# Two-layer attention and expert network on one core: transposes, values and output transposes a unit apart, and the layer 1 queries and keys projected earlier

## The chip, the cores and the metric

The kernel runs on one core of a Trainium2 chip, as one program in one launch. The metric is the device time of that launch in microseconds (us), as the median of several runs. The engines are TensorE (PE; its weight loads are shown apart, as PEld), VectorE (DVE), ScalarE (ACT), GpSimd (POOL) and SyncE (SP), whose queue issues nearly all transfers.

## The reference, cut to what matters

256 latent tokens and 256 context tokens of width 1024 go through two layers. Each layer is a modulated norm, a mixer with attention, an output projection with a gated residual, and then a network of 16384 experts, which takes most of the time and which the change leaves alone. Layer 0 mixes by neighbourhood attention (8 heads) beside window attention (8 heads); layer 1 by latent attention (8 heads, queries and keys made from small normed vectors) beside differential attention (4 heads, each the difference of two softmaxes and a norm of its own):

```python
# layer 0, head by head
p = softmax(q @ k.T * scale + bias)          # latents see latents and context, context sees context
y = p @ v
# layer 1, latent heads ("c")
q = rmsnorm(cq, gq) @ w_uq;  kv = rmsnorm(ckv, gkv) @ w_ukv
y_c = softmax(q_mla @ k_mla.T * 96**-0.5) @ v
# layer 1, differential heads ("d")
o1, o2 = softmax(q1 @ k1.T / 8) @ v, softmax(q2 @ k2.T / 8) @ v
y_d = rmsnorm(o1 - lam * o2, g) * (1 - lam_init)
```

## The kernel before, in words

All of it is float32 or a float32 made of two parts: a product with weights is three matmuls (`mm3`, L191 to L193: high by high, high by low, low by high). Weights come as one stream in the order of use: `take` starts the load of the blocks to come on SP's queue (L162) and has the next block split into its two parts by ACT (L167) and DVE (L168). The split parts have six buffers, three pairs.

**Layer 1, projections** (`mixer1`). First come the shared rotary key (block `("cdin", 0)`) and `proj_n("ckv")`, which keeps four PSUM banks, one for each block of 128 tokens. PSUM has eight banks: four single ones under the tag `b`, which `self.ps()` hands out, and two pairs under `s2`, which in the mixers hold the scores. A loop over the four token blocks then norms what lies in those banks: a square on ACT (L605, L608), a factor by DVE and POOL (`rstd`, L309 and L311), the scaling on DVE (L607, L610) into `nat`. Eight transposes of `nat` (L229, `p<-ck,nat`) and their copies follow, then the projections of the differential queries `dq` (four blocks of 24 matmuls with 256 columns) and keys `dk` (four blocks with 512 columns), each into a bank from `self.ps()`, copied and rotated (`rope`, L378, with the rotation's matmul L389 and DVE's L391 to L393 coming one block later), then the values `dv` and the products of the normed latents.

**Attention.** A unit is a pair of heads (one differential head in "d") by 128 queries: 32 units in layer 0, 16 in layer 1. A unit goes through `unit_s` (scores of both heads into one `s2` pair; head 0 uses rows 0 to 63 of the PE array and head 1 rows 64 to 127; L527 in layer 0, L707 and for the rotary part L713 in layer 1), `unit_p` (maximum on DVE, L443 or L446, exponentials on ACT, L454), `unit_n` (division by the sum, DVE) and `unit_y`. `unit_y` transposes the probabilities (`flip`, L229, `p<-ck,P`, four transposes into one bank, copied to SBUF as `PT` by ACT, L479, or for the second head by DVE, L477), multiplies them by the values (L560 in layer 0; L739 for "c" and L745 for "d" in layer 1) and writes the result in two parts. A "d" unit goes on: square on ACT (L749), factor on DVE and POOL, scaling on DVE (L751, tile `o`), another transpose on PE (L229, `p<-ck,o`), and the two parts by ACT and DVE (L755 to L757).

The units are pipelined in program text: iteration i issues `unit_s` of i, `unit_p` of i-1, `unit_n` of i-2 and the whole `unit_y` of i-3. Between them a filler hands in pieces of the modulation vectors of later use (L245, L260, L269, 512 KB weight blocks from SP's queue): one piece an iteration in layer 0, two in layer 1, both ahead of `unit_p`. The tile framework then fixes one order for each engine: the program text is its preference, an instruction that it expects to be ready may go ahead of one that isn't, and on the chip each engine follows that order. After the last unit `out_proj` multiplies by the output weights, blocks 0 and 1 with the rows of the first kind of heads ("a" or "c"), blocks 2 and 3 with those of the second.

Of the kernel before, what the change touches and what calls it, by code (L numbers as in the profile page):

```python
# [18 lines left out]
PSUM = bass.MemoryType.PSUM  # L19
# [17 lines left out]
YLAG = (3, 3)  # L37
# [38 lines left out]
class Phase:  # L76
    """a pool whose tags have a set number of buffers"""
# [13 lines left out]
class Kernel:  # L91
# [103 lines left out]
    def proj_t(self, key, hh, hl, c=512, **kw):  # L195
        """[128 columns, c tokens] in PSUM"""
        if key in self.pre:
            return self.pre.pop(key)
        w = self.take(key, **kw)
        p = self.ps()  # L200
        if not isinstance(w, tuple):
            self.product8(p[:, :c], w)
            return p
        wh, wl = w
        for k in range(8):
            b = slice(k * 128, (k + 1) * 128)
            self.mm3(p[:, :c], wh[:, b], wl[:, b], hh[:, k, :c], hl[:, k, :c], k == 0, k == 7)
        return p

    def product8(self, out, w):  # L210
        """the same in float32, of the modulated norm kept whole"""
# [3 lines left out]
    def proj_n(self, name, hh, hl, width, nt=4):  # L215
        """natural layout: nt banks [128 tokens, width]"""
# [15 lines left out]
    def ada_mm(self, l, v, half, pool):  # L232
        """half of one modulation vector for both conditions, in rows 0 and 1 of each 32 as four partial sums"""
# [80 lines left out]
    def squares(self, x, half, ss, junk):  # L314
        """sum of squares of one half of a token block; with the second the factor of the norm"""
# [6 lines left out]
    def norm_mod(self, xs, rst, l, vsh, vsc, keys, mid=None):  # L322
        """modulated norm, transposed; the projections of keys go along with it"""
# [52 lines left out]
    def rope(self, x, p, perm, cos, sin, n):  # L376
        """x [128, n] from p in PSUM, its first 256 columns (the latents) rotated, the rotation after the next one"""
# [59 lines left out]
    def probs1(self, P, S, scale, sink=None, bias=None):  # L437
        """P [128, 2, nk] <- exp of the two heads' scores less their maximum; sums in sm"""
# [31 lines left out]
    def flip(self, x, nk, eng):  # L470
        """[128, 128 nk] -> [128 keys, nk, 128]"""
# [11 lines left out]
    def mixer0(self, xs, sq):  # L483
# [67 lines left out]
        def unit_y(kind, c, qs, ctx, P):  # L551
            nk = 2 if ctx else 4
            y = self.ps([128, 128])
            PT = [self.flip(P[:, s], nk, s) for s in range(2)]
# [14 lines left out]
        S, P, N = {}, {}, {}  # L569
        for i in range(n + YLAG[0]):  # L570
            if i < n:
                S[i] = unit_s(*units[i])
            next(filler, None)
# [4 lines left out]
            if 0 <= i - YLAG[0] < n:  # L578
                unit_y(*units[i - YLAG[0]], N.pop(i - YLAG[0]))
# [5 lines left out]
    def mixer1(self, xs, sq):  # L585
# [10 lines left out]
        # cq | ckv in natural layout  # L596
        ckv = self.proj_n("ckv", hh, hl, 384)
        nat = []
        for t in range(4):
# [12 lines left out]
            self.rope_end()  # L612
        qnh = self.m.t("h2", [128, 2, 256], R, name="qnh")
# [21 lines left out]
        # kr (replicated), dq, dk transposed  # L635
        dq, dk = [], []
        for b in range(4):
            if b % 2 == 0:
                pair = self.m.t("h2", [128, 2, 256], name="dqp")
            x = pair[:, b % 2, :]  # L640
            self.rope(x, self.proj_t(("cdin", 1 + b), hh, hl, c=256), *r64, 256)
            dq.append(x)
        for b in range(4):
            if b % 2 == 0:
                pair = self.m.t("q4", [128, 2, 512], name="dkp")
            x = pair[:, b % 2, :]
            self.rope(x, self.proj_t(("cdin", 5 + b), hh, hl), *r64, 512)
            dk.append(x)
# [4 lines left out]
        # latent queries, keys and values  # L653
# [77 lines left out]
        def unit_y(kind, c, qs, P):  # L731
            PT = [self.flip(x, 4, i) for i, x in enumerate(P)]
# [18 lines left out]
            nc.vector.tensor_scalar(o[:, 1, :], y, rs, None, op0=OP.mult)  # L751
            y2 = self.ps([128, 128])
# [6 lines left out]
        units = [(kind, c, qs) for c in range(4) for kind in "cd" for qs in range(2)]  # L759
        n = len(units)  # L760
        S, P, N = {}, {}, {}
        for i in range(n + YLAG[1]):
            if i < n:
                S[i] = unit_s(*units[i])
            for _ in range(2):
                next(filler, None)
# [4 lines left out]
            if 0 <= i - YLAG[1] < n:  # L771
                unit_y(*units[i - YLAG[1]], N.pop(i - YLAG[1]))
# [5 lines left out]
    def top16(self, V, X, a, b):  # L778
        """sorted top 16 of each a, b as scratch, interleaved over the lists"""
# [12 lines left out]
    def route_scores(self, l, T, nd, hh, hl):  # L792
        """sorted top 16 of each half key for the dense blocks; scores of a further block go to DRAM"""
# [44 lines left out]
    def route(self, sv, al):  # L838
        """experts i, j and gates of one token block; a generator, leaves them in self.rt"""
# [64 lines left out]
    def gates(self, go, ti, G):  # L904
        """gate matrix of 128 tokens -> DRAM; a generator"""
# [66 lines left out]
    def peer(self, l, xs, sq, nd):  # L972
        """nd dense token blocks; a further block, if any, goes by gathered rows; returns the pieces of f"""
# [51 lines left out]
        # routing and gate matrix, with the first products of the main loop in between  # L1025
# [72 lines left out]
        def gather(n0, n1, after=None):  # L1098
            """rows of slots n0..n1, not before after is there"""
# [70 lines left out]
        def pace(j):  # L1170
            """slots used by the end of iteration j, even in time"""
# [31 lines left out]
    def residual(self, l, f):  # L1203
        """x + g2 f, in a new mixer phase"""
# [28 lines left out]
    def run(self):  # L1233
# [35 lines left out]
        # lambda of the differential heads, gain of its norm  # L1269
# [30 lines left out]
        # final norm  # L1300
# [159 lines left out]
```

## Time and profile before

| what | value |
|---|---|
| time, median of 3 runs | 2739.62 us |
| lowest and highest run | 2728.51 and 2740.89 us |
| span of the profiled execution, the only time the page has of it | 2734.2 us |
| PE, PEld busy | 95%, 83% of the span |
| DVE, ACT, POOL busy | 69%, 46%, 19% |
| attention of layer 0 | from about 147 to 267 us |
| layer 1: wait after `proj_n("ckv")`; attention | from 1670 to 1679 us; from 1750 to 1860 us |

The profile is of one execution. A busy time counts an instruction from its start to its modelled end, and matmuls overlap, so a stretch in which PE is busy all the time can still have starts that lie further apart than they need to. In the timeline a row gives start, duration, engine, line, operation, output and inputs, shapes and how many instructions were merged; in brackets the idle time just before it and what ended that.

### The profile page before, as it was taken

To read this page: it belongs to the slowest core of one execution; us is meant where nothing else is said; L and a number is where in the kernel's file an instruction comes from. 1 tells how busy PE (TensorE), PEld (TensorE's weight loads), DVE (VectorE), ACT (ScalarE), POOL (GpSimd) and SP (SyncE) were. 2 spreads that over 40 slices of the span, in tenths; PEclk is the share of its full clock that TensorE was granted. 3 is DMA by queue.
4 is the path that set the end of the run, shared out by engine and by line. 5 is a ranking of instruction groups with operands and counts; after the bars stand their busy time and mean duration, and the time that the engine had idled before them with its cause. 6 is when DMAs were issued, how large, how long until landed. Compare 5 with 4: busy or idle time off the path is not lost.

```text
span 2734.2 us, 43073 instructions
## 1 busy us (share of the span) xinstructions
PE 2610.7 (95%) x16265; PEld 2261.8 (83%) x16265; DVE 1876.3 (69%) x3862; ACT 1267.3 (46%) x2201; POOL 529.2 (19%) x534
## 2 busy tenths in 40 slices
PE   7999998989999999999999989998999999999998
PEld 6866787878899999999899767757999899999986
DVE  4267588886977777777777765365997565555455
ACT  3255335997333333333333333343499444444454
POOL 0000000000045555566565530000000000000000
PEclk9999999999999999999999998998999999999999
DMA  7262323977688888888888862453467976565355
GB/s 291 101 216 86 111 88 128 287 235 246 232 313 311 308 315 306 316 299 321 294 309 288 275 225 75 164 195 113 144 215 242 318 267 210 208 211 214 130 193 183
DMA packets 240977, 614.15 MB, mean 225 GB/s; under 512 B 18384, under 2 KB 102608, under 8 KB 240768
## 3 DMA queue, kind: packets, MB, share of 16 engines
q1 hardware_dynamic: 203904, 477.17, 50.6%
q0 software_dynamic: 36864, 134.23, 13.9%
q8 instruction: 127, 2.08, 0.3%
q14 instruction: 82, 0.67, 0.1%
HBM read 558.90 MB, written 52.43 MB: 224 GB/s over the span
## 4 chain that ended last, share of the span: by engine, by line
PE 62%; DVE 6%; DMA 3%; ACT 3%; issue 2%; POOL 1%; SPq 0%; DVEq 0%; POOLq 0%; ACTq 0%
PE p L192 19%; PE p L191 19%; PE p L193 19%; DMA gr<-in_v,ix 1%; PE p L213 1%; PE s L707 1%; PE p L229 1%; DVE ws L168 1%; ACT stage L957 1%; ACT og L940 1%; DVE vs L168 1%; DMA sc<-sd 1%; PE p L954 1%; ACT ws L167 1%; PE p L245 0%
## 5 line engine op out<-in xcount | busy, mean ns | idle before, releaser
L167 ACT CAST ws<-w 128x1024 fp32r<-128x1024 f32 (+1 forms) x327 | 343.0, 1050 | 634.0 <-PE p L192 581.4
L168 DVE TENSOR_TENSOR ws<-w,ws 128x1024 fp32r<-128x1024 f32 (+1 forms) x327 | 397.5, 1216 | 267.7 <-ACT ws L167 267.4
L192 PE MATMUL p<-vs,w 128*128 128x512 f32 x1280 | 502.2, 393 | 7.5 <-DVE vs L168 7.5
L167 ACT CAST vs<-v 128x1024 fp32r<-128x1024 f32 x256 | 269.5, 1053 | 509.5 <-PE p L192 509.5
L191 PE MATMUL p<-vs,w 128*128 128x512 f32 x1280 | 499.6, 391 | 4.4 <-ACT vs L167 4.4
L193 PE MATMUL p<-vs,w 128*128 128x512 f32 x1280 | 501.6, 392 | 0.0
L191 PE MATMUL p<-hh,ws 128*128 128x384 f32 (+2 forms) x1336 | 472.2, 354 | 6.2 <-ACT ws L167 2.9
L193 PE MATMUL p<-hh,ws 128*128 128x384 f32 (+2 forms) x1336 | 466.0, 349 | 1.5 <-DVE ws L168 1.5
L192 PE MATMUL p<-hl,ws 128*128 128x384 f32 (+2 forms) x1336 | 466.6, 349 | 0.0
L168 DVE TENSOR_TENSOR vs<-v,vs 128x1024 fp32r<-128x1024 f32 x256 | 312.8, 1222 | 152.7 <-ACT vs L167 151.0
L191 PE MATMUL p<-hp,ws 128*128 128x256 f32 x1032 | 295.5, 287 | 1.8 <-ACT ws L167 1.1
L193 PE MATMUL p<-hp,ws 128*128 128x256 f32 x1032 | 292.8, 284 | 0.8 <-DVE ws L168 0.8
L192 PE MATMUL p<-hp,ws 128*128 128x256 f32 x1032 | 293.2, 284 | 0.0
L192 PEld LDWEIGHTS p<-vs,w 128*128 128x128 f32 x1280 | 241.3, 189 | 56.5 <-DVE vs L168 11.1
L193 PEld LDWEIGHTS p<-vs,w 128*128 128x128 f32 x1280 | 240.9, 188 | 53.7 <-DVE w L1153 3.0
L191 PEld LDWEIGHTS p<-vs,w 128*128 128x128 f32 x1280 | 241.1, 189 | 50.6 <-ACT vs L167 4.6
L191 PEld LDWEIGHTS p<-hh,ws 128*128 128x128 f32 x1336 | 255.0, 191 | 24.7 <-ACT ws L167 4.3
L192 PEld LDWEIGHTS p<-hl,ws 128*128 128x128 f32 x1336 | 254.6, 191 | 14.9 <-issue 0.5
L193 PEld LDWEIGHTS p<-hh,ws 128*128 128x128 f32 x1336 | 254.5, 190 | 13.1 <-DVE ws L168 2.0
L1123 DVE SCALAR_TENSOR_TENSOR acc<-gr,ga,acc 128x1024 f32<-128x1024 f32 x128 | 164.2, 1283 | 102.3 <-DMA gr<-in_v,ix 101.7
L1118 DVE SCALAR_TENSOR_TENSOR gr<-gr,hn 128x1024 f32<-128x1024 f32 x128 | 156.2, 1224 | 108.5 <-DMA gr<-in_u,ix 102.5
L311 POOL TENSOR_TENSOR rso<-rsm,mhalf 128x1 f32<-128x1 f32 x30 | 20.1, 671 | 1079.4 <-DVE rsm L309 1079.4
(267 smaller groups left out, 4127.6 us busy)
## 6 DMA issues: line engine op xcount, KB each, us to landing
w<-in_uT SPq DMA_DIRECT2D x256, 512.0 KB
v<-in_v SPq DMA_DIRECT2D x256, 512.0 KB
w<-in_ada_w SPq DMA_DIRECT2D x96, 512.0 KB
G<-stage SPq DMA_DIRECT2D x40, 1024.0 KB
g<-G SPq DMA_DIRECT2D x32, 768.0 KB
w<-in_wq SPq DMA_DIRECT2D x32, 512.0 KB
g<-G SPq DMA_DIRECT2D x32, 512.0 KB
w<-in_w_out SPq DMA_DIRECT2D x16, 512.0 KB
```

What stands on the lines that cost most here:

```text
L167: self.nc.scalar.copy(hi, raw)
L168: self.nc.vector.tensor_tensor(lo, raw, hi.bitcast(F), op=OP.subtract)
L191: m(out, lh, rh, start=start, stop=False)
L192: m(out, lh, rl, start=False, stop=False)
L193: m(out, ll, rh, start=False, stop=stop)
L213: self.nc.tensor.matmul(out, w[:, k * 128:(k + 1) * 128], self.h32[:, k, :], start=k == 0, stop=k == 7)
L229: self.nc.tensor.transpose(out, x, self.ck("ident"))
L707: nc.tensor.matmul(S[:, s, :], a[c][h, q], b[c][h, :], start=True, stop=kind == "d", tile_position=(64 * s, 0))
L940: nc.scalar.activation(og_[:, 1, g, :, b], oh[:, 1, g, :, b], AF.Copy, scale=gl[:, k:k + 1])
L954: nc.tensor.matmul(p[:, k, :], oh[:, 0, g, :, b], og_[:, w, g, :, b], start=(w == 0), stop=(w == 1))
L1118: nc.vector.scalar_tensor_tensor(t, t, 1.0, hn, op0=OP.mult, op1=OP.mult, accum_out=ga[:, 0, n:n + 1])
L1123: nc.vector.scalar_tensor_tensor(acc, t, ga[:, 0, n - 128:n - 127], acc, op0=OP.mult, op1=OP.add)
```

## The change

In both mixers `unit_y` is cut: `unit_f` does the transposes and copies for unit i-3, and the product with the values is done for unit i-4, an iteration later. In layer 1 the second transpose of "d" units and what follows it become `unit_o`, for unit i-5. The loops run one iteration (layer 0) and two iterations (layer 1) longer. Layer 0's filler is called between `unit_f` and `unit_y`; in layer 1 one of the two calls moves there. In layer 1 each head group goes "d" first, then "c". The projections of `dq` and `dk` go ahead of the transposes of `nat`; `dq` is accumulated in `s2` pairs (argument `p` of `proj_t`) and its tiles come from the tag `q4` in place of `h2`. The rest of the diff takes comments out.

```diff
-    def proj_t(self, key, hh, hl, c=512, **kw):
+    def proj_t(self, key, hh, hl, c=512, p=None, **kw):
...
-        p = self.ps()
+        p = self.ps() if p is None else p
...
 # mixer0
-        def unit_y(kind, c, qs, ctx, P):
+        def unit_f(kind, c, qs, ctx, P):
+            return [self.flip(P[:, s], 2 if ctx else 4, s) for s in range(2)]
+
+        def unit_y(kind, c, qs, ctx, PT):
             nk = 2 if ctx else 4
             y = self.ps([128, 128])
-            PT = [self.flip(P[:, s], nk, s) for s in range(2)]
...
-        for i in range(n + YLAG[0]):
+        for i in range(n + 4):
             if i < n:
                 S[i] = unit_s(*units[i])
-            next(filler, None)
             if 0 <= i - 1 < n:
                 P[i - 1] = unit_p(*units[i - 1], S.pop(i - 1))
             if 0 <= i - 2 < n:
                 N[i - 2] = unit_n(*units[i - 2], *P.pop(i - 2))
-            if 0 <= i - YLAG[0] < n:
-                unit_y(*units[i - YLAG[0]], N.pop(i - YLAG[0]))
+            if 0 <= i - 3 < n:
+                X[i - 3] = unit_f(*units[i - 3], N.pop(i - 3))
+            next(filler, None)
+            if 0 <= i - 4 < n:
+                unit_y(*units[i - 4], X.pop(i - 4))
...
 # mixer1, right after the loop over nat; the same lines go out behind the transposes of nat
+        dq, dk = [], []
+        for b in range(4):
+            if b % 2 == 0:
+                pair = self.m.t("q4", [128, 2, 512], name="dqp")[:, :, :256]
+                p2 = self.pq.t("s2", [128, 2, 512])
+            x = pair[:, b % 2, :]
+            self.rope(x, self.proj_t(("cdin", 1 + b), hh, hl, c=256, p=p2[:, b % 2]), *r64, 256)
+            dq.append(x)
+        for b in range(4):
+            if b % 2 == 0:
+                pair = self.m.t("q4", [128, 2, 512], name="dkp")
+            x = pair[:, b % 2, :]
+            self.rope(x, self.proj_t(("cdin", 5 + b), hh, hl), *r64, 512)
+            dk.append(x)
...
-                pair = self.m.t("h2", [128, 2, 256], name="dqp")
...
-        def unit_y(kind, c, qs, P):
-            PT = [self.flip(x, 4, i) for i, x in enumerate(P)]
+        def unit_f(kind, c, qs, P):
+            return [self.flip(x, 4, i) for i, x in enumerate(P)]
+
+        def unit_y(kind, c, qs, PT):
             y = self.ps([128, 128])
...
             nc.vector.tensor_scalar(o[:, 1, :], y, rs, None, op0=OP.mult)
+            return o
+
+        def unit_o(kind, c, qs, o):
+            if o is None:
+                return
+            dst = slice(qs * 128, qs * 128 + 128)
             y2 = self.ps([128, 128])
             self.transpose(y2, o[:, 1, :])
...
-        units = [(kind, c, qs) for c in range(4) for kind in "cd" for qs in range(2)]
+        units = [(kind, c, qs) for c in range(4) for kind in "dc" for qs in range(2)]
...
-        for i in range(n + YLAG[1]):
+        for i in range(n + 5):
             if i < n:
                 S[i] = unit_s(*units[i])
-            for _ in range(2):
-                next(filler, None)
+            next(filler, None)
             if 0 <= i - 1 < n:
                 P[i - 1] = unit_p(*units[i - 1], S.pop(i - 1))
             if 0 <= i - 2 < n:
                 N[i - 2] = unit_n(*units[i - 2], *P.pop(i - 2))
-            if 0 <= i - YLAG[1] < n:
-                unit_y(*units[i - YLAG[1]], N.pop(i - YLAG[1]))
+            if 0 <= i - 3 < n:
+                X[i - 3] = unit_f(*units[i - 3], N.pop(i - 3))
+            next(filler, None)
+            if 0 <= i - 4 < n:
+                Y[i - 4] = unit_y(*units[i - 4], X.pop(i - 4))
+            if 0 <= i - 5 < n:
+                unit_o(*units[i - 5], Y.pop(i - 5))
```

## Rows read from the trace of the kernel before

**Rows 1.** The page's part 1: busy us, share of the span, instructions.

```profile
PE 2610.7 (95%) x16265; PEld 2261.8 (83%) x16265; DVE 1876.3 (69%) x3862; ACT 1267.3 (46%) x2201; POOL 529.2 (19%) x534
```

**Rows 2.** The page's part 4: the chain that ended last, by engine.

```profile
PE 62%; DVE 6%; DMA 3%; ACT 3%; issue 2%; POOL 1%; SPq 0%; DVEq 0%; POOLq 0%; ACTq 0%
```

**Rows 3.** Stretches: length, busy us of PE, PEld, DVE, ACT, POOL; clock; DMA share.

```profile
180.00:216.00 36.00, 35.60 (x372) 22.43 (x370) 26.15 (x87) 18.12 (x59) 1.05 (x2) 1.00 0.55 196
...
1670.00:1680.00 10.00, 5.11 (x19) 3.03 (x17) 5.54 (x16) 3.07 (x13) 3.09 (x6) 0.62 0.24 83
...
1750.00:1842.00 92.00, 83.72 (x868) 48.49 (x867) 54.03 (x123) 37.98 (x99) 6.96 (x13) 0.97 0.59 213
1842.00:1860.00 18.00, 12.53 (x80) 9.09 (x79) 9.02 (x27) 7.49 (x22) 1.09 (x2) 0.78 0.08 31
```

**Rows 4.** Timeline of PE from the end of `proj_n("ckv")` into block 1 of `dq`.

```profile
1670.09 0.34 PE L193 MATMUL p<-ws,hl 128*128 128x384 f32 x1
1672.45 1.16 PE L389 MATMUL p<-kr,ck 128*128 128x256 f32 x2 [2.03 <-DVE nat L610]
...
1678.64 0.56 PE L191 MATMUL p<-hh,ws 128*128 128x256 f32 x1
...
1682.80 0.28 PE L191 MATMUL p<-hh,ws 128*128 128x256 f32 x1
1682.92 0.28 PE L192 MATMUL p<-hl,ws 128*128 128x256 f32 x1
```

**Rows 5.** Timeline of DVE there: the splits of the `dq` blocks' weights.

```profile
1667.21 1.23 DVE L168 TENSOR_TENSOR ws<-w,ws 128x1024 fp32r<-128x1024 f32 x1 [2.94 <-ACT ws L167]
...
1672.22 1.22 DVE L168 TENSOR_TENSOR ws<-w,ws 128x1024 fp32r<-128x1024 f32 x1
```

**Rows 6.** Groups of PE by line, 1750 to 1860 us: busy, mean ns, idle before.

```profile
L745 PE MATMUL p<-dv,PT 128*128 128x128 f32 x64 | 10.3, 309 | 3.7 <-ACT PT L479 3.6
...
L229 PE MATMUL p<-ck,o 128*128 128x128 f32 x8 | 2.9, 365 | 7.2 <-DVE o L751 5.4 <-DVE rc L467 1.6
```

**Rows 7.** Timeline of PE in the middle of layer 1's attention.

```profile
1785.36 0.60 PE L229 MATMUL p<-ck,P 128*128 128x128 f32 x4
1786.63 1.16 PE L745 MATMUL p<-dv,PT 128*128 128x128 f32 x8 [0.68 <-ACT PT L479]
```

**Rows 8.** Timeline of PE at the end of layer 1's attention.

```profile
1855.74 2.08 PE L745 MATMUL p<-dv,PT 128*128 128x128 f32 x8 [0.73 <-ACT PT L479]
1859.47 0.47 PE L229 MATMUL p<-ck,o 128*128 128x128 f32 x1 [1.66 <-DVE o L751]
...
1863.59 0.43 PE L191 MATMUL p<-ws,hh 128*128 128x512 f32 x1
...
1864.31 0.39 PE L191 MATMUL p<-ws,hh 128*128 128x512 f32 x1
1864.54 0.39 PE L192 MATMUL p<-ws,hh 128*128 128x512 f32 x1
```

**Rows 9.** Waits, 147 to 268 us: us in total, times, longest.

```profile
PEld p L560 <- ACT PT L479: 15.5, 27, 0.8
...
PE p L560 <- ACT PT L479: 1.3, 4, 0.4
```

**Rows 10.** Timeline of PE in layer 0's attention.

```profile
183.15 1.12 PE L527 MATMUL s<-qk 64*128 64x512 f32 x2
184.20 1.09 PE L560 MATMUL p<-PT,av 128*64 128x128 f32 x16
185.22 1.12 PE L527 MATMUL s<-qk 64*128 64x512 f32 x2
...
188.31 1.13 PE L527 MATMUL s<-qk 64*128 64x512 f32 x4
189.37 1.09 PE L560 MATMUL p<-PT,av 128*64 128x128 f32 x16
```

More of the change, by code (lines that the diff above doesn't have):

```diff
@@ L36 @@
 AGRP = (2,)
-YLAG = (3, 3)
 ADA_WAIT = 2
@@ L568, in mixer0 @@
         n = len(units)
-        S, P, N = {}, {}, {}
-        for i in range(n + YLAG[0]):
+        S, P, N, X = {}, {}, {}, {}
+        for i in range(n + 4):
             if i < n:
                 S[i] = unit_s(*units[i])
-            next(filler, None)
             if 0 <= i - 1 < n:
@@ L634, in mixer1 @@
         nc.vector.tensor_tensor(kvl, kf, kvh.bitcast(F), op=OP.subtract)
-        dq, dk = [], []
-        for b in range(4):
-            if b % 2 == 0:
-                pair = self.m.t("h2", [128, 2, 256], name="dqp")
[L640 to L648, printed above, removed]
         dv = [self.m.t("q4", [128, 2, 512], name="dv") for _ in range(2)]
@@ L757, in unit_y @@
             nc.vector.tensor_tensor(yl[:, 4 + c, dst], o[:, 2, :], yh[:, 4 + c, dst].bitcast(F), op=OP.subtract)
-        units = [(kind, c, qs) for c in range(4) for kind in "cd" for qs in range(2)]
+        units = [(kind, c, qs) for c in range(4) for kind in "dc" for qs in range(2)]
         n = len(units)
-        S, P, N = {}, {}, {}
-        for i in range(n + YLAG[1]):
+        S, P, N, X, Y = {}, {}, {}, {}, {}
+        for i in range(n + 5):
             if i < n:
                 S[i] = unit_s(*units[i])
-            for _ in range(2):
-                next(filler, None)
+            next(filler, None)
             if 0 <= i - 1 < n:
```

## The prediction

> **What bounds the kernel.** The page's part 1 comes first: PE is busy for 95% of the span [rows 1], and the chain that ended last is PE's for 62%, with DVE next at 6% [rows 2]. So a microsecond that PE gains in a mixer moves the end by about one, because the expert network behind it is PE's too. The change touches only the mixers, so the second view is the table of stretches: where does PE stand still, or run slowly, inside them? In layer 0's attention hardly at all (35.60 of 36 us busy, clock 1.00). In layer 1 there are three places: 1670 to 1680 us (5.11 of 10 us busy, clock 0.62), the attention (83.72 of 92) and its end (12.53 of 18, clock 0.78) [rows 3]. The timeline and the groups by line then say who waits for what there.
>
> **Part 1, `dq` and `dk` ahead of the transposes of `nat`.** PE's last `ckv` matmul starts at 1670.09 and ends at 1670.43; the first matmul of `dq` starts at 1678.64. That is 8.2 us, of which the first wait, 2.03 us, ends with DVE's L610, which gives a `ckv` bank back [rows 4]. What PE does in it has to be done later all the same: eight transposes, four of which take 0.60 us in a row at full rate [rows 7], so 1.2, and two rotation matmuls of 256 columns at 0.12 us, 0.2. Then the clock: from 1678.64 to 1682.80 PE starts 18 matmuls of `dq`, 0.23 us each, where later ones start 0.12 apart [rows 4]; the clock of this stretch is 0.62, a mixture of its two levels, 1.2 and 2.4 GHz [rows 3]. 18 times 0.12 is 2.2, so 2.0 us go here. Sum: 8.2 - 1.4 + 2.0 = 8.8 us.
>
> Can `dq` start at 1670.4? Its accumulation goes to `s2` pairs, which nothing holds before the first scores at 1750. The weights of its first two blocks are there: block 2's split ends at 1668.44 and block 3's at 1673.44 [rows 5], while block 3 would be wanted after two blocks of 24 matmuls at 0.12, at about 1676. The stream of weights keeps its order, so SP's queue sees the same loads; the moved transposes issue no DMA, and neither do the three activations and six DVE instructions behind them. Those were ahead of the ropes on ACT and DVE and are now behind them; their products are first wanted by `uq`, after `dv`, and the 96 matmuls of `dv` cover them. What is late next is the rotation of `kr`: if the fixed order has it early among `dq`'s matmuls, PE waits there for L610 as before, up to 2.03 us. Bounds: 0 (all of `nat` stays in front) and 8.8. I take 8.
>
> **Part 2, layer 1's attention.** Two waits are what the edit aims at. L745 stood 3.7 us behind the copies of its own transposes, and the "d" units' second transpose stood 7.2 us behind `o` and DVE [rows 6]. One instance: four transposes start at 1785.36 and are through at 1785.96, and the product starts at 1786.63, after 0.68 us of idling for the copy [rows 7]. In the new order a whole iteration lies between, some 5.75 us (92 us [rows 3] by 16 units), with the next scores and a piece of the filler; the norm of a "d" unit, for which PE idled 1.66 us at 1857.8 [rows 8], gets an iteration too. So 10.9 us of waits lose their cause. Against them stands the end, where no next unit covers: the last two units still go from transposes to copy to product, at 0.7 us each [rows 7], and part of the 5.4 us behind L751 comes from DVE being late with splits of output weights, which will make something else late: I leave 3 us. That "c" is now last takes the norm out of the last chain; its idle time is in the 10.9 already. The clock: between the starts at 1859.47 and 1863.59, 4.12 us, lie a transpose and nine matmuls of `out_proj`, 0.44 each, where later ones are 0.23 apart [rows 8]; nine times 0.21 is 1.9 us, given back if the end has fewer gaps. Sum: 10.9 - 3 + 1.9 = 9.8; I take 10. Bounds: 0, if each wait is replaced by one of the same length, and 12.8, with no rest.
>
> "d" ahead of "c" at the start is priced at nothing: PE is full with `uq` and `ukv` products while the "d" scores could already start. The longer loops add no instruction to PE; their last iterations have only the pieces that were in `unit_y`.
>
> **Part 3, layer 0.** PE's own idle time before L560 for a copy is 1.3 us; its weight loads waited 15.5 us in 27 places, mostly while an earlier matmul still ran [rows 9]. These bound the gain: 1.3 and 15.5. PE is busy for 35.60 of 36 us [rows 3], so the lower one is nearer; some product runs are also broken after the first pair because the second head's copy is late. I take 4. The filler moves by eight transposes; its loads from SP's queue and POOL's fills of its bias tile move with it and are wanted by nobody soon.
>
> One rule speaks for much more here. The Trainium skill (Perfetto Trace Analysis, Identifying the Most-Contended Engine) says that matmul busy time overstates how near PE is to its limit, and to judge by the share of weight loads. That share is 22.43 of 36 us [rows 3], so by this rule some 38% of the 120 us of this attention, 45 us as an estimate, would be open. The starts in the timeline don't bear it out: 16 products take 1.02 us and are followed at once [rows 10]. By the rule the sum would have room for 45 in place of 4; I keep 4.
>
> **Sum.** 8 + 10 + 4 = 22 us. The profiled span of 2734.2 would become 2712.2; that execution lies 5.4 us below the median of the runs, so against the median, 2739.6 - 22 = **2718 us**.
>
> **The rivals.**
>
> *The order run was already full* (0.08). Each engine's order is fixed ahead of the run with what is expected to be ready, and PE already slips scores between transposes and products [rows 10]. If that did all of it, the text's new order changes next to nothing: 2739. Against it: the waits of rows 6 are there in that order.
>
> *The waits stay, for want of banks* (0.22). The four `b` banks are unchanged, and a "d" unit now holds its three in three different iterations beside the filler's. Then parts 2 and 3 give nothing and part 1 its 8 or 9: 2731. For it: the wait in front of `dq` did end with a bank given back [rows 4]. Against it: in the attention the ones named are a copy and `o`, data and not a free bank [rows 6]. The Trainium skill has this as a rule (Perfetto Trace Analysis, Optimization Strategy): gaps that repeat can mean too little PSUM for the next tile. By that rule the gaps of rows 7 would outlive the change; the releasers named there speak for the data.
>
> *Slower: score pairs come apart* (0.10). The four score matmuls of a unit take 1.06 us together, as the heads use different rows of the array, but two of them alone take 1.05 also, so a pair with a product in between costs 1.05 us more [rows 10]. In the timeline 16 of layer 0's 32 units are split so (10 with 512 columns, 6 with 256, which I price at half), and 8 of layer 1's 16. The change gives PE products that are always ready, just what gets between. If all others split as well: 6 x 1.05 + 10 x 0.53 + 8 x 1.05, and 8 x 1.05 for L713: 28.4 us. With the gain of 22 that gives 2746, with part 1 alone 2760; it ends on the other side from 21 more split pairs on.
>
> *Faster still: they come together* (0.10). If the products no longer fall between heads, 18 x 1.05 and 6 x 0.53 us come back, 22.1: 2696.
>
> **How the numbers follow.** The forecast has a chance of 0.50 and, with part 1 from 7 to 9, part 2 from 3 to 13 and part 3 from 1 to 8, a range of its own of 2709 to 2728. The range has to reach the banks rival (2731) and the full order (2739), and 2704 takes in most of the forecast's upper bounds; what it leaves out is most of both split rivals, 0.15 to 0.2: 2702 to 2740. A measurement of this kernel can tell 0.5%, 13.7 us, from no change. Faster by that, below 2726: most of the forecast (0.44), the pairs together (0.10), a little of the banks (0.04): 0.58. Slower, above 2753: the pairs apart with less than 16 us gained, 0.08. The same: 0.34.
>
> **What would show it.** Part 1 is right if PE's starts go on within a microsecond after the last `ckv` matmul, with `dq` at 0.12 and the clock at 1.00 there; wrong if L389 or the transposes of `nat` come first. Part 2: L745 and `p<-ck,o` without idle time in the groups, and from the first scores to `out_proj` some 10 us less. Part 3: layer 0's attention 3 to 5 us shorter, product runs whole. The forecast fails if the runs of L527 and L707 by twos become many more or fewer, if the waits reappear at the scores (L707 behind L454) or at DVE, or if the time gained goes to waits for weights at the start of the experts.

## The result, and the profile after

The changed kernel takes **2692.13 us** (median of 4 runs, 2683.2 to 2698.7), the kernel before beside it 2737.36 us: ratio 0.9832, 95% interval 0.9807 to 0.9856. That is 45 us less, where 22 had been forecast; the time lies below the range of 2702 to 2740 and 4 us under the rival "they come together" (2696). The profiled execution has 2690.64 us and a span of 2688.9, 45.3 less than before. Its lines are numbered differently: the scores are L526 (layer 0) and L711 (layer 1; its rotary part is L717), the products L561, L745 ("c") and L751 ("d"), every transpose is L228, the filler L244, L259 and L268, the copies of the transposes L478 (ACT) and L476 (DVE).

First the page of the kernel after: part 1 (busy us, share, instructions) and the first line of part 4 (the chain that ended last).

```profile
PE 2574.6 (96%) x16265; PEld 2248.1 (84%) x16265; DVE 1870.6 (70%) x3862; ACT 1266.4 (47%) x2201; POOL 526.7 (20%) x534
...
PE 32%; DVE 3%; ACT 2%; issue 1%; DMA 0%; POOL 0%; SPq 0%; DVEq 0%; POOLq 0%; ACTq 0%
```

Against [rows 1] PE has the same 16265 instructions and the same share of a shorter span, but 36.1 us less of busy time. So most of the gain is busy time that went away, and only the rest idle time; the prediction had looked for it in idle time. (The chain's 32% is no fall in PE's weight: the shares listed now add up to 38%, those of [rows 2] to 77%.)

Where it went, by stages whose ends are read from PE's timeline: layer 0's attention (last matmul of `av` to the end of the last product), from the last `ckv` matmul to layer 1's first scores, and layer 1's attention (from there to the end of the last product):

```
us              before   after   difference   (part of the prediction)
up to av         143.4   142.4      -1.0
attention 0      123.7   111.5     -12.2      part 3, taken as 4
between         1383.6  1382.4      -1.2
ckv to scores     79.9    73.8      -6.1      part 1, taken as 8
attention 1      107.9    85.3     -22.6      part 2, taken as 10
the rest         876.4   874.0      -2.4
(first matmul of ckv to its last: 19.4 in both)
```

The two attentions as stretches, first of the kernel before, then of the kernel after (columns as in [rows 3]).

```profile
143.38:267.09 123.71, 121.31 (x1128) 73.71 (x1126) 94.42 (x327) 69.58 (x217) 2.10 (x4) 1.00 0.48 167
1749.95:1857.82 107.87, 95.78 (x944) 57.10 (x943) 62.55 (x147) 45.10 (x119) 7.51 (x14) 0.95 0.52 187
```

```profile
142.38:253.88 111.50, 104.17 (x1127) 68.08 (x1125) 91.38 (x327) 68.48 (x217) 2.11 (x4) 0.95 0.54 185
1729.55:1814.87 85.32, 81.91 (x946) 51.35 (x945) 61.30 (x150) 45.06 (x121) 8.04 (x15) 1.00 0.65 236
```

Layer 0's PE is busy for 17 us less in a stretch that is 12 shorter, with the same instructions. Layer 1 has 13.9 us less busy time, 8.7 less idle time, and the clock at 1.00 in place of 0.95. Which instructions got cheaper is in the groups by line (busy, mean ns, idle time before), here of the kernel before, layer 0 and then layer 1.

```profile
L527 PE MATMUL s<-qk 64*128 64x256 f32 (+1 forms) x124 | 43.5, 531 | 0.2 <-ACT P L454 0.2
...
L560 PE MATMUL p<-PT,bv 128*64 128x128 f32 x192 | 19.0, 284 | 1.4 <-ACT PT L479 0.9 <-DVE P L548 0.3
...
L560 PE MATMUL p<-PT,av 128*64 128x128 f32 x192 | 17.4, 283 | 0.5 <-ACT PT L479 0.4
...
L707 PE MATMUL s<-knp,qnp 64*128 64x512 f32 x32 | 15.9, 648 | 1.0 <-ACT P L454 1.0
...
L707 PE MATMUL s<-dkp,dqp 64*128 64x512 f32 x32 | 12.2, 703 | 0.5 <-ACT P L454 0.4
```

And the same groups of the kernel after, with those that answer to [rows 6].

```profile
L526 PE MATMUL s<-qk 64*128 64x256 f32 (+1 forms) x124 | 30.5, 544 | 1.1 <-ACT P L453 1.1
...
L561 PE MATMUL p<-PT,av 128*64 128x128 f32 x192 | 14.8, 292 | 0.8 <-DVE ar L250 0.7
...
L561 PE MATMUL p<-PT,bv 128*64 128x128 f32 x192 | 14.1, 283 | 0.1
...
L711 PE MATMUL s<-knp,qnp 64*128 64x512 f32 x32 | 11.3, 641 | 0.0
L751 PE MATMUL p<-dv,PT 128*128 128x128 f32 x64 | 9.1, 285 | 0.2 <-ACT PT L478 0.2
...
L711 PE MATMUL s<-dkp,dqp 64*128 64x512 f32 x32 | 9.0, 641 | 0.2 <-ACT P L453 0.2
...
L228 PE MATMUL p<-ck,o 128*128 128x128 f32 x8 | 2.4, 304 | 1.6 <-DVE ar L250 1.2 <-ACT o L755 0.4
```

The two waits of [rows 6] went from 3.7 to 0.2 and from 7.2 to 1.6 us, as meant. But the 124 score matmuls of layer 0 fell from 43.5 to 30.5 us busy at the same 0.53 to 0.54 us each: the same matmuls lie over each other more. The timeline of PE in layer 0's attention of the kernel after says how; it answers to [rows 10].

```profile
198.46 1.13 PE L526 MATMUL s<-qk 64*128 64x512 f32 x4
199.52 0.66 PE L228 MATMUL p<-ck,P 128*128 128x128 f32 x4
200.01 0.95 PE L268 MATMUL p<-ck,ar 128*128 128x2 f32 x8
200.89 1.09 PE L561 MATMUL p<-PT,av 128*64 128x128 f32 x16
201.91 0.70 PE L526 MATMUL s<-qk 64*128 64x256 f32 x4
```

The scores stand in fours, and the product stands behind the transposes and a piece of filler, not between two heads. In PE's fixed order the split pairs of layer 0 went from 10 (512 columns) and 6 (256) to 0 and 2, those of layer 1 from 8 to 2.

Last, PE's timeline behind `ckv`, which answers to [rows 4].

```profile
1655.70 0.33 PE L192 MATMUL p<-ws,hl 128*128 128x384 f32 x1
1655.87 0.28 PE L190 MATMUL s<-hh,ws 128*128 128x256 f32 x1
...
1656.70 0.28 PE L191 MATMUL s<-hl,ws 128*128 128x256 f32 x1
1658.06 0.67 PE L388 MATMUL p<-kr,ck 128*128 128x256 f32 x2 [1.08 <-DVE nat L613]
1658.38 0.47 PE L192 MATMUL s<-hh,ws 128*128 128x256 f32 x1
```

`dq` starts 0.17 us behind `ckv` at 0.12 us a matmul; then the rotation of `kr` makes PE wait 1.08 us for DVE.

### The profile page after: what moved, and what is told of

It reads as the page before. It is cut to its first block, busy times and chain, and to the rows that moved or that the text cites. A ratio compares the mean times of both kernels' runs of the same rounds, so it can differ in the third digit from the quotient of the medians.

```text
span 2688.9 us, 43066 instructions
## 1 busy us (share of the span) xinstructions
PE 2574.6 (96%) x16265; PEld 2248.1 (84%) x16265; DVE 1870.6 (70%) x3862; ACT 1266.4 (47%) x2201; POOL 526.7 (20%) x534
## 3 DMA queue, kind: packets, MB, share of 16 engines
q0 software_dynamic: 36864, 134.23, 14.2%
## 5 line engine op out<-in xcount | busy, mean ns | idle before, releaser
L190 PE MATMUL p<-hh,ws 128*128 128x384 f32 (+1 forms) x1304 | 462.2, 355 | 6.3 <-ACT ws L166 2.9
L192 PE MATMUL p<-hh,ws 128*128 128x384 f32 (+1 forms) x1304 | 455.7, 350 | 1.6 <-DVE ws L167 1.6
L191 PE MATMUL p<-hl,ws 128*128 128x384 f32 (+1 forms) x1304 | 456.6, 350 | 0.1
L190 PEld LDWEIGHTS p<-hh,ws 128*128 128x128 f32 x1304 | 247.9, 190 | 24.7 <-ACT ws L166 4.4
L191 PEld LDWEIGHTS p<-hl,ws 128*128 128x128 f32 x1304 | 247.7, 190 | 14.7 <-DVE hl L367 0.3
L192 PEld LDWEIGHTS p<-hh,ws 128*128 128x128 f32 x1304 | 247.3, 190 | 13.1 <-DVE ws L167 2.0
L1134 DVE SCALAR_TENSOR_TENSOR gr<-gr,hn 128x1024 f32<-128x1024 f32 x128 | 156.0, 1222 | 107.7 <-DMA gr<-in_u,ix 107.4
```

The source lines that it names most:

```text
L190: m(out, lh, rh, start=start, stop=False)
L191: m(out, lh, rl, start=False, stop=False)
L192: m(out, ll, rh, start=False, stop=stop)
L1134: nc.vector.scalar_tensor_tensor(t, t, 1.0, hn, op0=OP.mult, op1=OP.mult, accum_out=ga[:, 0, n:n + 1])
```

## The experiments

All times are of the stages above, from one profiled execution each; medians with an interval where there were several runs. Kernels that leave layer 0 as before have 123.7, 125.6, 123.7, 125.3, 126.8 and 126.8 us there, so a stage repeats within some 3 us; times the granted clock (to three figures) they are 123.4 to 123.9, so nearly all of that spread is the clock's. The granted clock is given beside each time.

```
kernel      attention 0, clock   ckv to scores   attention 1, clock   whole, us
before          123.7  1.00           79.9             107.9  0.95        2737 to 2743 (medians)
after           111.5  0.95           73.8              85.3  1.00        2692.1
l0_cut          109.5  1.00           78.9             107.4  0.95        2727.2
l0_lag4         125.4  1.00           79.3             107.9  0.96        2745.9 (one run)
l0_filler       122.7  1.00           79.1             121.1  0.84        2748.8 (one run)
split_l0        121.5  0.99           73.8              85.4  1.00        2705.0
far_l0          126.2  0.97           73.8              85.3  1.00        2710.0
proj_first      126.8  0.97           73.8             105.7  0.98        2733.0 (one run)
dq_banks        113.2  0.95           75.9              85.5  1.00        2695.6 (one run)
l1_cut          125.6  0.99           79.0             102.1  0.90        2732.2
l1_o            123.7  1.00           79.2             100.4  0.97        2726.0 (one run)
l1_dc           125.3  0.99           79.3             121.2  0.89        2752.9 (one run)
l1_cut_o        126.8  0.97           79.2              93.8  0.93        2731.2 (one run)
after_cd        112.1  0.95           73.8              87.3  0.98        2691.3 (one run)
pool_norm       109.6  0.98           73.9              85.5  1.00        2690.6
act_norm        110.0  1.00           73.8              86.3  1.00        2689.9
nofill_l0        88.2  1.00           73.9              85.4  1.00        2701.7 (one run)
```

**The theory** was that a score pair of 512 columns costs 1.05 us more when it stands apart, and that the cut between transposes and product is what lets pairs stay together: a product that waits for its own copies lets the next unit's first head go ahead and then, being earlier in the text, comes between the heads. **The rivals** were that the named waits are all there is to gain, and that the filler's place or the longer lag did it.

### Layer 0: which of the edits

**l0_cut**, the kernel before with the cut alone:

```diff
+            if 0 <= i - 3 < n:
+                X[i - 3] = unit_f(*units[i - 3], N.pop(i - 3))
-            if 0 <= i - YLAG[0] < n:
-                unit_y(*units[i - YLAG[0]], N.pop(i - YLAG[0]))
+            if 0 <= i - 4 < n:
+                unit_y(*units[i - 4], X.pop(i - 4))
```

> The kernel before with one edit: in layer 0 transposes and products are cut apart (unit_f for i-3, unit_y for i-4), the filler where it was. In the fixed order of PE all 32 score pairs are whole, against 16 split ones before. Theory of the pairs: a product that waits for its copies lets the next unit's first head go ahead and then comes in between; with the products a unit later none does. The stage of layer 0's attention (last av matmul to last product) goes from 123.7 to about 110 us (16 splits: 10 x 1.05 + 6 x 0.53 = 13.7 us) and the time down by 12 to 15. Theory of the waits: only the idle time behind copies goes, 2 to 4 us.

Measured: 109.5 us (14.2 less), ratio to the kernel before 0.9955 (0.9935 to 0.9976). The group of the scores in this kernel:

```profile
L527 PE MATMUL s<-qk 64*128 64x256 f32 (+1 forms) x124 | 28.2, 531 | 3.0 <-ACT P L454 3.0
```

The scores' busy time falls by 15.3 us (10 x 1.05 + 6 x 0.53 is 13.7), while the idle time before them rises by 2.8. The cut alone does all of layer 0's gain; that the changed kernel has 111.5 goes with its clock, 0.95 there and 1.00 here. It goes with the filler's place too: with at most two pairs apart, the three kernels with the filler at its new place (after, dq_banks, after_cd) have 111.5 to 113.2 us at 0.95, the three with it at its old place (this one, pool_norm, act_norm) 109.5 to 110.0 us at 0.98 to 1.00. So no gain of the filler's move, a part of the change, is seen in layer 0; no run takes that move alone out of the changed kernel.

**l0_lag4**, the uncut transposes and product a unit later (`YLAG = (4, 3)`):

> The kernel before with layer 0's unit_y as a whole an iteration later (i-4), not cut. 13 of 32 pairs are split in the fixed order (before 16). Theory of the pairs: transposes and their product still stand next to each other, so the stage stays within 3 us of 123.7. A rival, that it is the longer distance to the softmax that counts, expects it near 111.

Measured: 125.4. More time for the chain before the transposes is worth nothing.

**l0_filler**, the filler's piece moved between transposes and product, uncut:

> The kernel before with layer 0's filler called between the transposes and the product inside unit_y. 13 of 32 pairs split. Theory of the pairs: 3 pairs fewer, the stage 120 to 124 us. Rival, that any work between transposes and product is enough: 113 or less.

Measured: 122.7. The filler does not do it. (Its 121.1 us in layer 1, whose text is unchanged, is the clock: last section.)

### Is it the pairs, or the product that no longer waits?

**split_l0**, the changed kernel with the second head's scores issued behind the product:

```diff
                 unit_y(*units[i - 4], X.pop(i - 4))
+            if i < n:
+                unit_s(*units[i], heads=(1,), S=S[i])
```

> The changed kernel with the second head's scores of layer 0 issued behind the iteration's product, so that 14 pairs of 512 columns and 12 of 256 are split in the fixed order (changed kernel: none and 2). Theory of the pairs: 14 x 1.05 + 10 x 0.53 = 20 us more, stage 111.5 to about 131, time about 20 above the changed kernel. Rival, a split costs nothing because other work fills the time: stage within 3 us of 111.5.

Measured: 121.5, 10 more; ratio to the kernel before 0.9882 (0.9842 to 0.9921). It is neither the 20 of the theory nor the rival's 0 to 3. The timeline of PE in this kernel says why:

```profile
203.44 1.12 PE L527 MATMUL s<-qk 64*128 64x512 f32 x4
204.49 0.66 PE L228 MATMUL p<-ck,P 128*128 128x128 f32 x4
205.08 1.08 PE L244 MATMUL p<-w,cs 128*32 128x128 f32 x32
206.09 0.66 PE L563 MATMUL p<-PT,av 128*64 128x128 f32 x8
206.67 0.70 PE L527 MATMUL s<-qk 64*128 64x256 f32 x4
```

The second head of one unit now stands beside the first head of the next, and a run of four is again over after 1.05 us. There are 12 such runs with columns of 512 (in 6 of them, the one shown too, two of the four matmuls have 256) and 8 runs of two, where the kernel before has 5 and 20. Two heads share the time whichever units they belong to. So a test was wanted in which nothing stands beside either.

**far_l0**, the changed kernel with the second head's scores behind the transposes, ahead of filler and product:

```diff
                 X[i - 3] = unit_f(*units[i - 3], N.pop(i - 3))
+            if i < n:
+                unit_s(*units[i], heads=(1,), S=S[i])
             next(filler, None)
```

> The changed kernel with one edit in layer 0: the second head's scores of a unit are issued behind the transposes of an earlier unit, so that the two heads stand apart and no other head's scores stand beside either. In the fixed order 13 pairs of 512 columns and 12 of 256 are apart (0 and 2 in the changed kernel); products stay a unit behind their transposes. Theory of the pairs, at the prices that the prediction read from the timeline: 13 times 1.05 and 10 times 0.53, 19 us more than 111.5 in layer 0's attention, less at most the some 7 us for which PE stands idle there: 123 to 131 us. Rival, the cut between transposes and product is what made layer 0 faster and the pairs only came along: 110 to 115 us.

Measured: 126.2, 14.7 more than the changed kernel; ratio to the kernel before 0.9876 (0.9851 to 0.9901). Its timeline and the stretch:

```profile
199.43 1.12 PE L527 MATMUL s<-qk 64*128 64x512 f32 x2
200.48 1.09 PE L228 MATMUL p<-ck,P 128*128 128x128 f32 x8
201.50 1.12 PE L527 MATMUL s<-qk 64*128 64x512 f32 x2
202.55 1.09 PE L563 MATMUL p<-PT,av 128*64 128x128 f32 x16
```

```profile
142.37:268.61 126.24, 122.23 (x1127) 73.91 (x1125) 93.93 (x327) 69.17 (x217) 2.10 (x4) 0.97 0.48 164
```

With the cut in place and only the pairs apart, layer 0's attention is as long as before the change (times the clock 122.8 us, 123.7 before). Added up from each run's start to the next run's start, the scores take 48.5 us here, 31.6 in the changed kernel and 40.8 in the kernel before: 17.0 more for 23 pairs that came apart, priced at 18.95. This settles layer 0: the gain is the pairs, and the cut is how they were brought together.

### Part 1

**proj_first**, the kernel before with `dq` and `dk` first:

> The kernel before with one edit: layer 1's dq and dk projected straight behind ckv, dq into the score banks. Theory: from the last ckv matmul to dq 0.2 us (8.55 before), to the first scores 73 to 75 us (79.9 before), attention as before (106 to 109 us): 6 us less in all. Rival, the 6 us came with the attention's new order, or are given back there as later work waits for nat and its transposes: from the last ckv matmul to the end of the last product 186 us or more (187.8 before).

Measured: 73.8 and 105.7, together 179.5 (187.8 before). The 6 us are part 1's own, and 2.2 more come in the attention, whose clock is 0.98 in place of 0.95 (last section).

**dq_banks**, the changed kernel with `dq` in the common banks:

```diff
-                p2 = self.pq.t("s2", [128, 2, 512])
-            self.rope(x, self.proj_t(("cdin", 1 + b), hh, hl, c=256, p=p2[:, b % 2]), *r64, 256)
+            self.rope(x, self.proj_t(("cdin", 1 + b), hh, hl, c=256), *r64, 256)
```

> The changed kernel with one edit: dq accumulates in the four common banks in place of the score banks. Theory: those four are held by ckv until DVE and ACT have read them, so dq starts 2 to 8 us behind the last ckv matmul (0.17 in the changed kernel), with a lower clock behind the gap, and the first scores come 76 to 80 us behind it (73.8 in the changed kernel, 79.9 before). Rival, the order alone makes the gain, the banks come free in time: under 75 us.

Measured: 75.9, just under the theory's range; `dq` starts 3.83 us behind the last `ckv` matmul. The timeline of PE there:

```profile
1659.48 0.34 PE L192 MATMUL p<-ws,hl 128*128 128x384 f32 x1
1661.84 0.67 PE L388 MATMUL p<-kr,ck 128*128 128x256 f32 x2 [2.03 <-DVE nat L613]
1663.31 0.36 PE L190 MATMUL p<-hh,ws 128*128 128x256 f32 x1 [0.80 <-DVE rt L390]
```

The wait of [rows 4] is back with its 2.03 us: 2.1 of part 1's 6.1 us are the score banks, the other 4 the order.

### Layer 1: the parts alone and together

**l1_cut**, the kernel before with product, norm and second transpose a unit behind the transposes:

> The kernel before with one edit in layer 1's attention: the probability transposes stay three units behind the scores, product, norm and second transpose go a unit later; filler, unit order and everything else as before. Stage: from the first scores to the end of the last product 107.9 us before, 85.3 in the changed kernel. Theory of the pairs and waits: the fixed order has 3 of 16 score pairs split in place of 8 (5 us at 1.05 each), the product's own waits (3.7 us) go, and with fewer gaps the clock of the last part is higher (1 to 2 us): 97 to 99 us. Rival, the idle time that the groups name is all there is: only L745's 3.7 us, so 104 us, and whatever the pairs do is hidden. Second rival, the second transpose is what holds everything: no change, 106 to 109 us.

**l1_o**, the kernel before with only the second transpose later:

> The kernel before with one edit: the second transpose of the differential units (and what follows it) a unit later; transposes and product still together. Theory of the pairs and waits: 6 of 16 pairs split in place of 8 (2 us), most of the 7.2 us before the second transpose go: from the first scores to the end of the last product 98 to 101 us (107.9 before). Rival, the norm's chain only moves its wait to DVE or to the next product: 105 to 108 us.

**l1_dc**, only the units' order:

> The kernel before with one edit: in layer 1 the differential units of a pair of heads come ahead of the latent ones. Theory of the pairs: the fixed order has 12 of 16 pairs split in place of 8, 4 us at 1.05, and 2 us less at the end, where the last unit has no norm: 108 to 112 us from the first scores to the end of the last product (107.9 before). Rival, the order of the units is worth a part of the gain by itself: 102 us or less.

Measured: 102.1, 100.4 and 121.2 us: between theory and rival, as the theory said, and far above both. The clocks differ (0.90, 0.97, 0.89). A way to compare them is an estimate that takes PE to be the limit: length times mean granted clock. For the four kernels with layer 1's attention as before that gives 102.5, 102.0, 103.6 and 101.7 us, though their lengths run from 107.4 to 121.1, so it takes most of the clock out. By it l1_cut has 91.9 (10.6 less than 102.5), l1_o 97.3 (5.2 less) and l1_dc 107.9 (5.4 more, where 4 for the pairs less 2 at the end were expected).

One row of l1_cut says what is late next, the second transpose [rows 6]:

```profile
L229 PE MATMUL p<-ck,o 128*128 128x128 f32 x8 | 2.6, 326 | 10.6 <-DVE rc L467 7.0 <-DVE o L753 3.6
```

Its idle time rose from 7.2 to 10.6 us. That led to **l1_cut_o**, both edits together:

> The kernel before with two edits in layer 1's attention together: product a unit behind its transposes, second transpose a unit behind that; the latent units first and the filler where it was. In the fixed order 1 of 16 pairs split (8 before). Alone the two gave 5.8 and 7.5 us, and with the first alone PE stood 10.6 us before the second transpose (7.2 before). Theory, each alone leaves a wait that the other removes: the two together 86 to 90 us from the first scores to the end of the last product, 18 to 22 less than 107.9. Rival, they add up: 94.6, so 93 to 97 us, and the filler's place makes the rest.

Measured: 93.8 at clock 0.93: the rival's figure. Times the clock it is 87.3, 15.2 less, and 10.6 + 5.2 is 15.8. So they add up, and the theory that each needs the other falls. What single lengths hid was the clock. The 2.0 us that are left to the 85.3 of the kernel after were not taken apart.

**after_cd**, the changed kernel with "c" ahead of "d" again:

> The changed kernel with one edit: in layer 1 the latent units of a pair of heads come ahead of the differential ones again, as in the kernel before. The fixed order has no score pair of layer 1 split (2 in the changed kernel, 8 before). Theory of the pairs and waits: 1 to 2 us for the pairs, against it some 2 us at the end, where the last unit has a norm again: 84 to 88 us from the first scores to the end of the last product (85.3 in the changed kernel). Rival, putting the differential units first is what lets the rest work: over 92 us.

Measured: 87.3, in the theory's range. The order of the units is worth 2 us net: two pairs fewer stand apart, but PE idles for 6.8 us in place of 3.4, half of the rise in the last 21 us, where the theory had it, and half in one wait of 2.15 us for a piece of the filler near the start.

### What holds layer 0's attention now

DVE is busy for 91.4 of its 111.5 us, so two attempts to go further took work from DVE, both with the filler at its old place.

**pool_norm**, half of the normalisation on GpSimd (`(nc.gpsimd if s else nc.vector).tensor_scalar(...)` in `unit_n`):

> The changed kernel with two edits in layer 0's attention: the filler's piece stands between scores and exponentials again, as before, and the second head's multiplication by the reciprocal sum (32 instructions, 415 ns each on DVE) runs on GpSimd. Theory, DVE is what holds this attention now (93% busy from 216 to 240 us): 109.5 us with the filler's old place alone, 12 of DVE's 92 us less, so 103 to 107 us; all in all 4 to 8 us under the changed kernel. Rival, PE's own work or the chain of one unit holds it: 108 to 111 us. Second rival, GpSimd takes several times DVE's time or slows DVE down: over 112 us.

**act_norm**, the same for the 16 units of 256 keys on ACT:

> The changed kernel with two edits in layer 0's attention: the filler's piece stands between scores and exponentials again, as before, and in the 16 units of 256 keys the second head's multiplication by the reciprocal sum runs on ACT in place of DVE. Theory, DVE is what holds the second half of this attention: 16 times 0.3 to 0.4 us less for it, 106 to 109 us (109.5 with the filler's old place alone). Rival, ACT's exponentials are on the same chain and get later: 109 to 112 us.

Measured: 109.6 and 110.0 us, 2690.62 (ratio 0.9831, 0.9802 to 0.986) and 2689.94 us (0.9828, 0.98 to 0.9855): no gain over l0_cut's 109.5, and within 3 us of the changed kernel. DVE's busy time did fall, from 91.4 to 85.2 and 88.0 us, but the stage did not follow. Both theories fall. The groups of pool_norm:

```profile
L547 POOL TENSOR_SCALAR P<-P,rc 128x512 f32<-128x512 f32 (+1 forms) x32 | 42.7, 1334 | 161.9 <-DVE rc L466 138.8 <-PE p L228 11.7 <-PE s L526 4.0
...
L547 DVE TENSOR_SCALAR P<-P,rc 128x512 f32<-128x512 f32 (+1 forms) x32 | 15.1, 473 | 1.1
```

**nofill_l0**, the changed kernel with the filler behind layer 0's attention:

> The changed kernel with the filler's pieces of layer 0's attention all issued behind it, so that PE has some 21 us less to do inside (the transposed products of the modulation). Theory, PE itself still sets the length of this attention: 88 to 94 us (111.5 in the changed kernel). Rival, DVE and the chain of one unit set it, as DVE has some 88 us of work left: 100 us or more, and the pieces behind it cost their 21 us on top.

Measured: 88.2 us, and 37.8 more until `out_proj` starts. The stretches, attention and filler:

```profile
143.20:231.50 88.30, 79.89 (x706) 50.26 (x709) 82.49 (x314) 62.20 (x210) 0.00 (x0) 1.00 0.15 49
231.50:269.30 37.80, 26.50 (x425) 18.90 (x425) 4.99 (x11) 4.69 (x7) 2.10 (x4) 0.78 0.91 340
```

Taking some 21 us of PE's work out (26.5 us busy at 0.78 in the second row) makes it 23 shorter, while DVE lost only 8.9: PE still sets the length, and only without the filler would DVE (82.5 of 88.3 us) be next. The best of all runs and the changed kernel can't be told apart.

## Why the prediction was wrong

**The step that failed** is the price of the score pairs. The forecast's sum held them at nothing, as two rivals of 0.10 each, and the pairs that came together are worth about 12 us in layer 0 (shown) and 6 in layer 1 (priced by rows).

**Part 1 was right, with 6.1 us for 8.** The gap went from 8.55 to 0.17 us and `dq` runs at full clock from the start, as worked out. Of the 1.9 us that are missing, 1.08 are the wait that the prediction named as next, at the rotation of `kr`.

**Part 3 failed at "These bound the gain: 1.3 and 15.5", and at the choice of the lower one because "PE is busy for 35.60 of 36 us".** Busy time counts a pair that stands apart as two spells of work. 16 split pairs lay inside those 35.60 us. A stage that was busy for 98% of its time held 12 us of room, and l0_cut and far_l0 show it to be the pairs' room. The stretch shown in [rows 3] reads nearly as full in the kernel after, because 6.8 us of it run at the lower clock level there (0.91 in the mean); l0_cut, the second row, runs it at 1.00 and is less full, with 414 matmuls where the kernel before has 372:

```profile
180.00:216.00 36.00, 34.85 (x390) 23.53 (x388) 28.93 (x100) 20.55 (x64) 1.05 (x2) 0.91 0.62 219
180.00:216.00 36.00, 33.34 (x414) 22.88 (x412) 30.18 (x104) 21.99 (x67) 1.05 (x2) 1.00 0.68 237
```

The rule on the share of weight loads (the Trainium skill, Perfetto Trace Analysis, Identifying the Most-Contended Engine), which the prediction set aside, says that matmul busy time is no good measure of how near PE is to its limit. This trace agrees: 98% busy, and 12 us to gain. But the estimate of 45 us worked out from the share was not reached, and the share itself hardly moved (73.71 of 123.71 us to 68.08 of 111.50, 60% to 61%) while 12 us went.

**Part 2 was right in its mechanism and short in its sum.** The two waits gave 9.1 of the 10.9 us (3.7 to 0.2, 7.2 to 1.6). The clock's 1.9 us were of the stretch just behind this stage, which has 1.00 in the kernel after. Inside the stage, for which the sum had no clock, length times clock goes from 102.5 to 85.3, so by this estimate 5.4 of the 22.6 us are the clock's. Six pairs that came together are 6.3 more at 1.05, the price in this stage's timeline before as well, where a run of four is over after 1.06 us and a run of two after 1.05:

```profile
1758.14 1.13 PE L707 MATMUL s<-dkp,dqp 64*128 64x512 f32 x4
1759.20 1.08 PE L245 MATMUL p<-w,cs 128*32 128x128 f32 x32
...
1780.88 1.12 PE L707 MATMUL s<-dkp,dqp 64*128 64x512 f32 x2
1781.93 1.16 PE L745 MATMUL p<-dv,PT 128*128 128x128 f32 x8
1783.02 1.12 PE L707 MATMUL s<-dkp,dqp 64*128 64x512 f32 x2
```

The three make 20.8 of 22.6; no run splits pairs alone in layer 1, so this division is worked out, not shown. The bound of 12.8 failed because it held only waits that a row names and the clock of one stretch.

**The direction of the pairs was wrong.** The sentence that failed stands in the slower rival: "The change gives PE products that are always ready, just what gets between." It is the other way round. A product that must still wait for its own copies gets between; that l0_cut has no split pair and l0_lag4 still 13 is measured, that the wait is what opens the place is argued from the orders, not shown. The rival "they come together" had the mechanism and the price (22.1 us) and only 0.10 of chance. That its time came within 4 us is in part luck: by stages it has 17.7, 18.4 and 8 us where 12.2, 22.6 and 6.1 were measured, and 4.6 us came outside these stages. The price held up: 1.05 us from one pair of rows [rows 10], 17.0 of 18.95 us in far_l0; only the half price for 256 columns was low, as a run of two is over after 0.63 us there. The Trainium skill (TensorE: Matmul & The Clock Gate, Part 3, The mechanism) says that matmuls in different rows of the array overlap and that matmuls are not reordered; the trace agrees (four in 1.06 us, two in 1.05, and a product between two heads is not overtaken), and put beside the split pairs it would have named the room.

**The rivals that fell.** The waits did not outlive the change for want of banks in the attention, with the same four `b` banks; behind `ckv` a bank did matter, as dq_banks shows (2.1 us).

## What to carry to other kernels

Where matmuls in different rows of the array can run side by side, count in the engine's order how many stand apart: that time is inside "busy" and no wait names it. An edit that gives a waiting instruction its inputs early can gain most by where it then falls in the order, so compare the orders of before and after for what now stands next to what. And before stage times of single profiles are set against each other, multiply them by the granted clock where PE is the limit, or a few microseconds of clock will pass for an effect.

## What the runs showed of the hardware that was not expected

The same layer-1 attention took 107.9 us in one execution and 121.1 in another (kernel before, l0_filler); the difference is the clock, 0.95 against 0.84. One place where it falls is common to many kernels: 12 to 14 us behind the first scores PE stands 1.00 us for ACT and 0.79 for DVE, and then runs partly at the lower level. The stretches there, of the kernel before:

```profile
1755.00:1760.00 5.00, 5.00 (x75) 2.52 (x74) 3.03 (x6) 3.38 (x9) 0.42 (x1) 1.00 0.97 359
1760.00:1765.00 5.00, 3.21 (x20) 1.01 (x10) 3.16 (x7) 1.45 (x4) 0.00 (x0) 0.97 0.92 356
1765.00:1770.00 5.00, 5.00 (x30) 3.10 (x30) 2.55 (x7) 2.47 (x7) 0.53 (x1) 0.69 0.44 169
```

And of l1_cut, where it stays down:

```profile
1772.40:1777.40 5.00, 2.51 (x19) 0.65 (x9) 2.45 (x7) 1.45 (x4) 0.00 (x0) 0.90 0.93 344
1777.40:1782.40 5.00, 5.00 (x12) 2.70 (x12) 3.27 (x7) 2.61 (x6) 0.53 (x1) 0.50 0.46 176
1782.40:1787.40 5.00, 5.00 (x49) 2.66 (x52) 2.10 (x6) 0.68 (x3) 0.00 (x0) 0.50 0.07 10
```

12 and 49 matmuls run in 5 us there, at 0.50 of full speed (1.2 GHz), in stretches that read as wholly busy. All eight kernels with the old order of projections dip at this place, in two to four stretches of 5 us; the nine with `dq` and `dk` first do not. That is a second gain of part 1 which the prediction did not have. In the kernel before it is 1.7 us by the rows above (5 us at 0.97 and 5 at 0.69); the larger part of the loss, some 4 us, is at the end of the attention, 18 us at 0.78 [rows 3]. What brings the dip about stays open: proj_first has nearly the same two waits at this place (1.00 and 0.57 us) and no dip.

In pool_norm GpSimd took 1334 ns in the mean (its spans are rough) for a multiplication that takes DVE 415, and DVE's own half of them slowed to 473 ns.
